# A hybrid decoder layer on one core: factor steps spread over more matrix units, gated rows in two buffers, other units in seven products, longer step counts in the retention

## The chip, the cores and the metric

The kernel runs on one core of a Trainium2 chip, in float32. The metric is the device time of one execution in microseconds (us). Five engines work at once, each with an instruction stream of its own: TensorE (PE, the matrix products; PEld is its weight loading), VectorE (DVE), ScalarE (ACT), GpSimd (POOL) and SyncE (SP, whose queue issues nearly all transfers). In the code they are `PE`, `V`, `A`, `G_` and `SP`. An instruction waits until what it reads has been written and what it overwrites has been read; those behind it on its engine wait too.

## What is computed

520 columns go through one layer: 512 prompt tokens and 8 single-token samples.

```python
proj = rmsnorm(x) @ w_in                        # q, k, v, g of the retention; q, k, v of the attention; two gates
o_r  = retention(rotary(q_r), rotary(k_r), v_r) # 4 heads, 256 wide keys, 512 wide values; state S = gamma*S + k^T v
a    = (group_norm(o_r) * silu(g_r)) @ w_pa
b    = dilated_attention(q_a, k_a, v_a) @ w_pb  # 12 heads
h    = x + (sigmoid(gate_a) * a + sigmoid(gate_b) * b) @ w_o
u, w = split(rmsnorm(h) @ w_ffn_in)             # hidden width 2816 = 22 blocks of 128
y    = rmsnorm(h + (silu(u) * w) @ w_ffn_out)
```

For each of the 8 samples the retention also reads its state (256 x 512 in each of the 4 heads), updates it and writes it back.

## The kernel before

**Columns and products.** Activations stand transposed: features on the 128 partitions, 520 columns along the free dimension, in two halves of 260 (`HF`). Each float32 factor is split in a high part (ACT, a copy to the matrix format) and a low part (DVE, the difference), and a product is three matmuls: high by high, high by low, low by high. Weights come as a stream `wall` of 512 KB pieces in the order of use (line 167). Each block of 512 columns of weights is split by `block_hi`: high part `wh` on ACT (line 200), low part `wl` on DVE (line 203); `advance` keeps this five blocks ahead of the product.

**Units.** `unit` (line 250 for its matmuls) makes one block of 128 output rows: for each of the k blocks of its input, 3 matmuls for each half, and then one `pump()`. The results of consecutive units lie in two pairs of accumulator banks (`pm`), so a unit can start when the results of the unit before the last one have been read.

**Seven-product units.** `quad` (line 306 for its matmuls) makes two output blocks, over two input halves and two column halves, by seven block products where the plain way has eight. For this it needs sums of weight blocks (`qq`, lines 184 to 190, on DVE) and seven factors of the input. Each of its seven steps has 12 matmuls and two pumps, so a quad has 14 pumps. The results of some steps are copied out by ACT (line 312, tiles `s12` and `s35`) and put together by DVE.

**Pumps.** There is no scheduler: instructions stand on each engine in the order in which Python issues them. Side work is written as generators in queues: P (first), S and Q. Each pump first runs the calls that `later(n, ...)` put off by n pumps, and then takes one step of those queues that stand in the current entry of `pattern`: with `["PS", "P", "PS"]` the P queue steps at each pump and the S queue at two of three. A `yield` ends a step. The number of yields thus sets how much other work, and how many matmuls, lie between two pieces of side work.

**Retention.** Per head h, the units are q (2), k (2), and then g (4) and v (4), for heads 0 and 3 v before g. On the P queue run `gen_scores` (the split of q and k, lines 490 and 491; the score matmuls, line 503; the decay factor, line 510), `gen_vT` and `gen_out` (the products with v, line 551; normalisation; the final state, line 569). On the S queue runs `gen_sample`: sixteen steps for the 8 samples and two halves of the state, each with an ACT product `kv` (line 619), a DVE update `st` (line 654), every other one with a DVE product `y` (line 635), loads of `state` (line 606) and of `vb` (line 611) and a store (line 624); after eight steps, and after sixteen, the `y` go through matmuls into `oacc` (line 664). The sample work of head h is started at the end of its v units, so that of head 2 runs beside the units of head 3.

**Feed forward.** 22 input units, `FFSEQ` in order; with unit i go the weights of both halves of SwiGLU. A plain one (`ffn_in`) is two units of 8 input blocks (16 pumps); those in `INQ` are quads (`ffn_in_quad`). After unit 8 and after unit 16 come four output quads (`ffn_out`), which use the gated rows of units 0 to 7, and 8 to 15; the rows of units 16 to 21 are used as they are at the end. The first three plain units use rows that aren't yet normed (`X2`); their results are multiplied with the row factor `rs2` (lines 1320 and 1329). The others use `XP`, and the quads also `XT`: these are the factors, which `gen_factors` makes on the P queue from the start of the feed forward. It makes the 8 blocks of `XP` (lines 1217, 1220, 1221) with two yields each, and then four groups of `XT` (lines 1232 to 1244) with six yields, the last one with five. The gated rows of a pair of units go to `UF` (`middle`; lines 1333 and 1360), one buffer; `right`, on the S queue, makes seven factors of them for the output quads (lines 1292 to 1303). `right` of the pair (0, 1) is pushed at unit 2 and is run to its end at once there (`finish`), because unit 2 writes to the same buffer; the other pairs' is pushed at the end of the odd unit and runs beside the unit after it.

Of the kernel before, what the change touches and what calls it, by code (L numbers as in the profile page):

```python
# [8 lines left out]
F32 = mybir.dt.float32  # L9
# [15 lines left out]
CHUNKS = ((0, 8), (8, 8), (16, 6))  # L25
LAST = [(c, k) for k0 in (0, 4) for c in range(2) for k in range(k0, min(k0 + 4, 6))]
LAST[8:] = [(0, 4), (1, 4), (0, 5), (1, 5)]
INQ = (6, 7, 9, 10, 11, 13, 14, 15, 17, 18, 19, 21)
FFSEQ = []
for (a_, n_), ahead_ in zip(CHUNKS, (1, 1, 0)):  # L30
    FFSEQ += [("in", i_, i_ in INQ) for i_ in range(a_ and a_ + 1, a_ + n_ + ahead_)]
    FFSEQ += [("out", c_, True) for c_ in range(0, 8, 2) if ahead_]
QUADS = {128 + 2 * i_: 4 for i_, e_ in enumerate(FFSEQ) if e_[2]}
GAMMA = [1.0 - 2.0 ** (-5.0 - h) for h in range(RH)]


@with_exitstack
def tile_hybrid_layer(
# [411 lines left out]
    for h in range(RH):  # L450
# [31 lines left out]
        def gen_scores(h, tens, Dt):  # L482
            kt = [rp.tile([128, 4, DK], F32R, tag="kt" + i, name="kt" + i) for i in "hl"]
            tens["kt"] = kt
            q, k = tens["q"], tens["k"]
            parts = []
            for x, i in ((q, "h"), (k, "l")):
                p = rp.tile([128, 4, T], F32R, tag="v" + i, bufs=1, name="p" + i)
                hi, lo = p[:, 0:2, :], p[:, 2:4, :]
                A.activation(hi, x, AF.Copy)  # L490
                later(3, lambda x=x, hi=hi, lo=lo: V.tensor_tensor(lo, x, f32(hi), op=ALU.subtract))
                parts.append((hi, lo))
                yield
            (qh, ql), (kh, kl) = parts
            for _ in range(3 if h else 8):
                yield
            for jb in range(4):
                n = T - 128 * jb
                sp = sbank()
                i0 = min(jb * 128, HT)  # L500
                mm = [(dt, x, y) for dt in range(2) for x, y in ((kh, qh), (kh, ql), (kl, qh))]
                for i, (dt, x, y) in enumerate(mm):
                    PE.matmul(sp[:, :T - i0], x[:, dt, jb * 128:(jb + 1) * 128], y[:, dt, i0:], start=i == 0,  # L503
                              stop=i == len(mm) - 1)
                yield
                sp = sp[:, jb * 128 - i0:]
                t = tmp("sc")
                o = SCO[jb] + (128 if jb == 3 else 0)
                hi, lo = scs[0][:, o:o + n], scs[1][:, o:o + n]
                V.tensor_tensor(t[:, :n], sp[:, :n], Dt[:, :n], op=ALU.mult)  # L510
                A.activation(hi, t[:, :n], AF.Copy)
                later(2, lambda hi=hi, lo=lo, t=t, n=n: V.tensor_tensor(lo, t[:, :n], f32(hi), op=ALU.subtract))
            tens["v"] = [rp.tile([128, 4, DV], F32R, tag="v" + i, bufs=1, name="v" + i) for i in "hl"]
            for jp in range(2):
                sp = sbank()
                for i in range(2):
                    for dt in range(2):
                        jb = 2 * jp + i
                        pe_T(sp[:, i * 256 + dt * 128:i * 256 + dt * 128 + 128], k[:, dt, jb * 128:(jb + 1) * 128])
                yield  # L520
                for i in range(2):
                    jb = 2 * jp + i
                    A.activation(kt[0][:, jb, :], sp[:, i * 256:(i + 1) * 256], AF.Copy, scale=kdec[:, h, jb:jb + 1])
                yield
                for i in range(2):
                    jb = 2 * jp + i
                    V.scalar_tensor_tensor(kt[1][:, jb, :], sp[:, i * 256:(i + 1) * 256], kdec[:, h, jb:jb + 1],
                                           f32(kt[0][:, jb, :]), op0=ALU.mult, op1=ALU.subtract)
# [13 lines left out]
        def gen_out(h, tens):  # L542
# [20 lines left out]
                                       tokv(tens["g"][:, c, :]), op0=ALU.mult, op1=ALU.mult)  # L563
            tens["gdone"] = True
            for dt in range(2):
                sp = sbank()
                for jb in range(4):
                    for x, y in three:
                        PE.matmul(sp, kt[x][:, jb, dt * 128:(dt + 1) * 128], v[y][:, jb, :], start=jb == 0 and x == y,  # L569
                                  stop=jb == 3 and x == 1)  # L570
                    if jb % 2:
                        yield
                sf = tmp("sf")
                A.activation(sf[:, :DV], sp, AF.Copy)
                yield
                later(2, lambda sf=sf, dt=dt: SP.dma_start(s_p[0, 0, h, dt * 128:(dt + 1) * 128, :], sf[:, :DV]))
# [16 lines left out]
        def gen_sample(h, tens):  # L593
# [57 lines left out]
            for i in range(2 * NS):  # L651
# [5 lines left out]
                later(1, lambda i=i, f=second if dt else first: f(i))  # L657
                yield
                if i % 8 == 7:
                    for _ in range(3):  # L660
                        yield
                    for bb in range(b - 3, b + 1):
                        j = bb % 4
                        PE.matmul(acc[32 * j:32 * j + 32, :], om[:, bb, :], ys[bb], start=b == 3, stop=b == NS - 1,  # L664
                                  tile_position=(0, 32 * j), skip_group_check=True)
                    yield
# [102 lines left out]
            g_units()  # L769
        push("P", gen_out(h, tens))  # L770
        before = tens
        pattern[:] = ["PS", "P", "PS"] if h == RH - 2 else ["P", "S", "P", "PS", "P", "S"]


    SG = {}
# [434 lines left out]

    def gen_factors():
        yield from gen_norm2()
        xs = {}

        def one(c, out):
            x = ftmp("xn")
            V.scalar_tensor_tensor(x, hT[:, c, :], g2v[:, c:c + 1], rs2, op0=ALU.mult, op1=ALU.mult)
            xs[c] = x
            hi, lo = (XP[:, i, c // 2, 1:3, :] if c % 2 else XP[:, i, c // 2, 0::3, :] for i in range(2))
            A.activation(hi, halves(x), AF.Copy)  # L1220
            later(2, lambda: V.tensor_tensor(lo, halves(x), f32(hi), op=ALU.subtract))

        for c in range(8):
            one(c, None)
            yield
            yield
        for k in range(4):
            x1, x2 = xs.get(2 * k), xs.get(2 * k + 1)
            if k < 3:
                x1, x2 = ftmp("xn"), ftmp("xn")  # L1230
                for c, x in ((2 * k, x1), (2 * k + 1, x2)):
                    V.scalar_tensor_tensor(x, hT[:, c, :], g2v[:, c:c + 1], rs2, op0=ALU.mult, op1=ALU.mult)
                yield
            t = fp.tile([128, 4, HF], F32, tag="ts", name="ts")
            V.tensor_tensor(t[:, 0, :], x1[:, :HF], x1[:, HF:], op=ALU.subtract)
            V.scalar_tensor_tensor(t[:, 1, :], x2[:, HF:], -1.0, t[:, 0, :], op0=ALU.mult, op1=ALU.subtract)
            V.tensor_tensor(t[:, 2, :], x2[:, HF:], x1[:, HF:], op=ALU.subtract)
            V.scalar_tensor_tensor(t[:, 3, :], t[:, 1, :], -1.0, x2[:, :HF], op0=ALU.mult, op1=ALU.subtract)
            yield
            for j in (0, 2):  # L1240
                hi, lo = XT[:, 0, k, j:j + 2, :], XT[:, 1, k, j:j + 2, :]
                A.activation(hi, t[:, j:j + 2, :], AF.Copy)  # L1242
                yield
                V.tensor_tensor(lo, t[:, j:j + 2, :], f32(hi), op=ALU.subtract)
                yield

    def xnsrc(k):
        return tuple((XP[:, i, k // 2, k % 2, :], XP[:, i, k // 2, 2 if k % 2 else 3, :]) for i in range(2))
# [8 lines left out]
    push("P", gen_factors())  # L1257

    UL = fp.tile([128, 28, HF], F32R, name="UL")
    UF = fp.tile([128, 8, HF], F32, name="UF")  # L1260
    NP = CHUNKS[2][0]
    NX = 3

    def snaps():
        return [fp.tile([128, 2, HF], F32, tag=t, bufs=b, name=t) for t, b in (("s12", 2), ("s35", 1))]

    def whole(i, t):
        hi, lo = (halves(u[:, i - NP, :]) for u in (UHp, ULp))
# [3 lines left out]
    def middle(i, mult):  # L1272

        if i > NP:
            t = halves(ftmp("fu"))
            mult(t)
            whole(i, t)
            return
        if i == NX - 1:
            rights.append(push("S", right(UF, 0)))  # L1280
        if i % 2 == 0 and rights:
            finish("S", rights[-1])
        mult(UF[:, 1:3, :] if i % 2 else UF[:, 0::7, :])
        if i % 2 and i > 1:
            rights.append(push("S", right(UF, i % 8 // 2)))

    rights = []

    def right(t, k):

        yield
        V.tensor_tensor(t[:, 3, :], t[:, 0, :], t[:, 7, :], op=ALU.subtract)
        V.scalar_tensor_tensor(t[:, 4, :], t[:, 2, :], -1.0, t[:, 3, :], op0=ALU.mult, op1=ALU.subtract)
        yield
        V.tensor_tensor(t[:, 5, :], t[:, 2, :], t[:, 7, :], op=ALU.subtract)
        V.scalar_tensor_tensor(t[:, 6, :], t[:, 4, :], -1.0, t[:, 1, :], op0=ALU.mult, op1=ALU.subtract)
        yield
        for j, n in ((0, 3), (3, 2), (5, 2)):
            hi, lo = (u[:, k, j:j + n, :] for u in (UH4, UL4))
            A.activation(hi, t[:, j:j + n, :], AF.Copy)  # L1300
            yield
            yield
            V.tensor_tensor(lo, t[:, j:j + n, :], f32(hi), op=ALU.subtract)
            yield

    def open_u():
        nonlocal UH4, UL4, UHp, ULp
# [77 lines left out]
    for kind, i, seven in FFSEQ:  # L1385
# [3 lines left out]
            ffn_out(i)  # L1389
            continue  # L1390
        if i == NP + 1:
            whole(NP, UF[:, 0::7, :])
        (ffn_in_quad if seven else ffn_in)(i)

    last = bpool.tile([128, 7 * D], F32, tag="bg", name="last")
# [216 lines left out]
```

## Time and profile before

| | us |
|---|---|
| median of 3 runs | 1319.31 (1316.19 to 1320.3) |
| the profiled execution | 1318.89 |
| its span, first to last instruction | 1317.1 |
| PE, PEld busy in the span | 1282.0, 1247.7 |
| DVE, ACT, POOL busy in the span | 820.3, 574.9, 83.2 |

In the answers about the trace a time is in us from the start of the span. A wait row names the engine, the tile and line of the waiting instruction, and behind the arrow what ended the wait; then the total, the number of waits and the longest. A row of the timeline has start, length, engine, line, operation, output and inputs, and in brackets the idle time of the engine before it. A window row has the window, its length, the busy time of each engine with the number of its instructions, the granted clock of PE (1.00 is full speed), the busy share of the transfer engines and GB/s.

### The profile page before, as it was taken

Reading aid. Unit: us, or ns where it says so; the run is one execution under the profiler, and the core shown is the slowest. Engines: PE = TensorE matmul, PEld = TensorE weight load, DVE = VectorE, ACT = ScalarE, POOL = GpSimd, SP = SyncE. Lnnn points to the kernel's source line nnn. Section 1 sums busy time; section 2 is a strip of 40 time slices with the busy share of each in tenths; the row PEclk is TensorE's granted clock in tenths of the full one; section 3 lists DMA queues with packets and bytes.
Section 4 is the critical chain, followed back from the end, with each engine's and each line's share of the span. In section 5 each row is a group of like instructions: output and inputs, shape, how many; then the busy total and the mean of one; then the engine's idle time right before and its main releaser. Section 6 shows DMA issues by size and latency. Waiting matters only on the chain.

```text
span 1317.1 us, 25670 instructions
## 1 busy us (share of the span) xinstructions
PE 1282.0 (97%) x10465; PEld 1247.7 (95%) x10465; DVE 820.3 (62%) x1735; ACT 574.9 (44%) x1100; POOL 83.2 (6%) x69
## 2 busy tenths in 40 slices
PE   8999999999999999999999999999979999999997
PEld 7999999998888999999999999899979999999997
DVE  7867636847655532234545455476697788879765
ACT  4564334534554522244434343233444556555532
POOL 3601001001002000000000000040000000000000
PEclk9999999999899999999999999999999999999999
DMA  6266235737575332445555455534222333233321
GB/s 219 83 233 228 93 113 196 245 119 233 170 267 182 95 92 87 136 126 152 157 161 164 138 173 177 204 121 128 74 62 83 97 113 113 76 101 113 97 81 66
DMA packets 89782, 183.35 MB, mean 139 GB/s; under 512 B 12024, under 2 KB 33944, under 8 KB 89664
## 3 DMA queue, kind: packets, MB, share of 16 engines
q1 hardware_dynamic: 88944, 180.64, 43.7%
q8 instruction: 82, 1.34, 0.4%
q10 hardware_dynamic: 720, 1.07, 0.2%
q14 instruction: 36, 0.29, 0.1%
HBM read 155.70 MB, written 25.98 MB: 138 GB/s over the span
## 4 chain that ended last, share of the span: by engine, by line
PE 85%; DVE 7%; DMA 2%; issue 2%; ACT 2%; POOL 1%; SPq 0%; DVEq 0%; ACTq 0%
PE pm L250 59%; PE pm L306 12%; PE sp L322 3%; PE pc L306 2%; DMA vb<-vd 2%; PE sp L551 2%; PE sp L569 2%; PE pm L1500 1%; DVE wl L203 1%; PE sp L961 1%; PE sp L503 1%; PE sp L911 1%; ACT wh L200 1%; PE oacc L664 1%; PE sacc L1106 1%
## 5 line engine op out<-in xcount | busy, mean ns | idle before, releaser
L250 PE MATMUL pm<-X,wh 128*128 128x260 f32 x3392 | 561.8, 288 | 8.1 <-ACT XT L1242 3.8
L250 PEld LDWEIGHTS pm<-X,wh 128*128 128x128 f32 x3392 | 470.2, 190 | 23.1 <-issue 8.3
L203 DVE TENSOR_TENSOR wl<-raw,wh 128x512 fp32r<-128x512 f32 x384 | 275.8, 720 | 169.6 <-ACT wh L200 165.8
L250 PE MATMUL pm<-X,wl 128*128 128x260 f32 x1696 | 342.7, 284 | 0.1
L200 ACT ACTIVATE wh<-raw 128x512 fp32r<-128x512 f32 x384 | 238.7, 625 | 211.0 <-PE pm L250 160.7
L250 PEld LDWEIGHTS pm<-X,wl 128*128 128x128 f32 x1696 | 262.9, 189 | 0.5 <-DVE wl L364 0.5
L250 PE MATMUL pm<-GA,wh 128*128 128x260 f32 x512 | 82.2, 283 | 0.0
L250 PE MATMUL pm<-XP,wh 128*128 128x260 f32 x448 | 72.2, 283 | 3.2 <-DVE fb L1329 1.9
L306 PE MATMUL pm<-XT,wh 128*128 128x260 f32 x384 | 71.9, 286 | 2.6 <-DVE UF L1360 1.7
L250 PEld LDWEIGHTS pm<-GA,wh 128*128 128x128 f32 x512 | 70.1, 189 | 0.0
L250 PEld LDWEIGHTS pm<-XP,wh 128*128 128x128 f32 x448 | 61.3, 188 | 3.6 <-issue 2.1
L306 PEld LDWEIGHTS pm<-XT,wh 128*128 128x128 f32 x384 | 59.1, 188 | 4.8 <-DVE UF L1360 2.7
L619 ACT ACTIVATE kv<-vb,ks 128x512 f32<-128x512 f32 x64 | 44.2, 714 | 29.2 <-DMA vb<-vd 28.8
L331 POOL TENSOR_TENSOR r<-v,cst 128x4 f32<-128x4 f32 (+4 forms) x14 | 17.6, 1259 | 595.5 <-DVE v L329 595.5
L306 PE MATMUL pm<-UH,wh 128*128 128x260 f32 x192 | 54.2, 282 | 0.0
L306 PE MATMUL pm<-UL,wh 128*128 128x260 f32 x192 | 54.2, 282 | 0.0
L306 PE MATMUL pm<-XT,wl 128*128 128x260 f32 x192 | 54.2, 282 | 0.0
L306 PE MATMUL pm<-UH,wl 128*128 128x260 f32 x192 | 54.1, 282 | 0.0
L654 DVE SCALAR_TENSOR_TENSOR st<-st,kv 128x512 f32<-128x512 f32 x64 | 45.4, 713 | 11.4 <-ACT kv L619 11.4
L250 PE MATMUL pm<-GA,wl 128*128 128x260 f32 x256 | 51.6, 283 | 0.0
L312 ACT ACTIVATE s<-pm 128x260 f32<-128x260 f32 x80 | 30.8, 386 | 45.6 <-PE pm L306 45.3
L200 ACT ACTIVATE wh<-qq 128x512 fp32r<-128x512 f32 x60 | 37.3, 629 | 30.4 <-PE pm L250 17.4
(322 smaller groups left out, 2100.1 us busy)
## 6 DMA issues: line engine op xcount, KB each, us to landing
raw<-wall SPq DMA_DIRECT2D x192, 512.0 KB
st<-state SPq DMA_DIRECT2D x64, 256.0 KB
out<-st SPq DMA_DIRECT2D x64, 256.0 KB
area<-ck SPq DMA_DIRECT2D x24, 512.0 KB
vb<-vd SPq DMA_DIRECT2D x32, 256.0 KB
area<-qd SPq DMA_DIRECT2D x12, 512.0 KB
cb<-cd SPq DMA_DIRECT2D x4, 768.0 KB
xr<-xT SPq DMA_DIRECT2D x8, 260.0 KB
```

The costliest lines, as they stand in the source:

```text
L200: A.activation(h, r, AF.Copy)
L203: V.tensor_tensor(l, r, f32(h), op=ALU.subtract)
L250: PE.matmul(pm[:, f, :HF], w, x[f] if isinstance(x, tuple) else x[:, f * HF:(f + 1) * HF], start=first, stop=last)
L306: PE.matmul(out[bank], w[:, ks], factor(i, k, x), start=bank not in begun, stop=k == nkp - 1 and w is l, skip_group_check=True)
L312: A.activation(snap[(0, 3, 1, None, 2)[j]], out[bank], AF.Copy)
L322: PE.transpose(out, in_, ident[:n, :n])
L331: G_.tensor_tensor(r[:rows, :ncol], v[:rows, :ncol], mhalf[:rows].to_broadcast([rows, ncol]), op=ALU.pow)
L503: PE.matmul(sp[:, :T - i0], x[:, dt, jb * 128:(jb + 1) * 128], y[:, dt, i0:], start=i == 0, stop=i == len(mm) - 1)
L551: PE.matmul(sp[:, i0:], v[x][:, jb, c * 128:(c + 1) * 128], scs[y][:, SCO[jb]:SCO[jb] + T - i0], start=jb == 0 and x == y, stop=jb == 3 an ...
L569: PE.matmul(sp, kt[x][:, jb, dt * 128:(dt + 1) * 128], v[y][:, jb, :], start=jb == 0 and x == y, stop=jb == 3 and x == 1)
L619: A.activation(kvs[i][:, :DV], vbs[b], AF.Copy, scale=ks[:, dt, b:b + 1])
L654: V.scalar_tensor_tensor(sts[i], sts[i], GAMMA[h], kvs.pop(i)[:, :DV], op0=ALU.mult, op1=ALU.add)
```

## The change

- `INQ`: the seven-product input units are 7, 8, 9, 11, 12, 13, 15, 16, 17, 19, 20, 21 in place of 6, 7, 9, 10, 11, 13, 14, 15, 17, 18, 19, 21: twelve as before. Units 8 and 16, ahead of the output quads, become quads; 6, 10, 14 and 18 become plain.
- `gen_factors`: four yields for each block of `XP` in place of two; thirteen for each group of `XT` in place of six; the last group makes its two normed rows again, as the others do, in place of keeping them.
- `UF`: two buffers of four rows in turn in place of one of eight, and a tile `us` for the four sums that `right` makes; `right` of (0, 1) isn't run to its end at unit 2 any more; one DVE operation to a step, and fewer yields for the last pair of a set of eight (k = 3). `s12` has one buffer in place of two.
- Retention: `gen_scores` waits 7, 7 and 6 steps in heads 1, 2, 3 in place of 3 before its matmuls (head 0: 8 as before); `gen_out` has one more yield ahead of each half of the final state; `gen_sample` has five yields ahead of the `oacc` matmuls in place of three; and beside the units of head 3 the S queue steps at three of four pumps in place of two of three.

```diff
-INQ = (6, 7, 9, 10, 11, 13, 14, 15, 17, 18, 19, 21)
+INQ = (7, 8, 9, 11, 12, 13, 15, 16, 17, 19, 20, 21)
+SCW = (8, 7, 7, 6)
...
-            for _ in range(3 if h else 8):
+            for _ in range(SCW[h]):
                 yield
...
             for dt in range(2):
+                yield
                 sp = sbank()
...
                 if i % 8 == 7:
-                    for _ in range(3):
+                    for _ in range(5):
                         yield
...
-        pattern[:] = ["PS", "P", "PS"] if h == RH - 2 else ["P", "S", "P", "PS", "P", "S"]
+        pattern[:] = ["PS", "PS", "P", "PS"] if h == RH - 2 else ["P", "S", "P", "PS", "P", "S"]
...
         for c in range(8):
-            one(c, None)
-            yield
-            yield
+            one(c)
+            for _ in range(4):
+                yield
         for k in range(4):
-            x1, x2 = xs.get(2 * k), xs.get(2 * k + 1)
-            if k < 3:
-                x1, x2 = ftmp("xn"), ftmp("xn")
-                for c, x in ((2 * k, x1), (2 * k + 1, x2)):
-                    V.scalar_tensor_tensor(x, hT[:, c, :], g2v[:, c:c + 1], rs2, op0=ALU.mult, op1=ALU.mult)
+            x1, x2 = ftmp("xn"), ftmp("xn")
+            for c, x in ((2 * k, x1), (2 * k + 1, x2)):
+                V.scalar_tensor_tensor(x, hT[:, c, :], g2v[:, c:c + 1], rs2, op0=ALU.mult, op1=ALU.mult)
                 yield
...
+            yield
             V.tensor_tensor(t[:, 2, :], x2[:, HF:], x1[:, HF:], op=ALU.subtract)
             V.scalar_tensor_tensor(t[:, 3, :], t[:, 1, :], -1.0, x2[:, :HF], op0=ALU.mult, op1=ALU.subtract)
+            yield
             yield
             for j in (0, 2):
                 hi, lo = XT[:, 0, k, j:j + 2, :], XT[:, 1, k, j:j + 2, :]
                 A.activation(hi, t[:, j:j + 2, :], AF.Copy)
                 yield
+                yield
                 V.tensor_tensor(lo, t[:, j:j + 2, :], f32(hi), op=ALU.subtract)
                 yield
+            yield
+            yield
...
+        if i % 2 == 0:
+            if len(rights) > 1:
+                finish("S", rights[-2])
+            UF[i // 2] = fp.tile([128, 4, HF], F32, tag="uf", bufs=2, name="uf")
+        t = UF[i // 2]
+        mult(t[:, 1:3, :] if i % 2 else t[:, 0::3, :])
         if i == NX - 1:
-            rights.append(push("S", right(UF, 0)))
-        if i % 2 == 0 and rights:
-            finish("S", rights[-1])
-        mult(UF[:, 1:3, :] if i % 2 else UF[:, 0::7, :])
-        if i % 2 and i > 1:
-            rights.append(push("S", right(UF, i % 8 // 2)))
+            rights.append(push("S", right(UF[0], 0)))
+        if i % 2 and i > NX - 1:
+            rights.append(push("S", right(t, i % 8 // 2)))
...
+        t = fp.tile([128, 4, HF], F32, tag="us", name="us")
+        V.tensor_tensor(t[:, 0, :], b[:, 0, :], b[:, 3, :], op=ALU.subtract)
+        yield
...
+        for x, j, n in ((b[:, 0:3], 0, 3), (t[:, 0:2], 3, 2), (t[:, 2:4], 5, 2)):
             hi, lo = (u[:, k, j:j + n, :] for u in (UH4, UL4))
-            A.activation(hi, t[:, j:j + n, :], AF.Copy)
-            yield
-            yield
-            V.tensor_tensor(lo, t[:, j:j + n, :], f32(hi), op=ALU.subtract)
-            yield
+            A.activation(hi, x, AF.Copy)
+            yield
+            if k < 3:
+                yield
+            V.tensor_tensor(lo, x, f32(hi), op=ALU.subtract)
+            if k < 3:
+                yield
```

More of the change, by code (lines that the diff above doesn't have):

```diff
@@ L1212, in gen_factors, with one @@
         yield from gen_norm2()
-        xs = {}
-        def one(c, out):
+        def one(c):
             x = ftmp("xn")
             V.scalar_tensor_tensor(x, hT[:, c, :], g2v[:, c:c + 1], rs2, op0=ALU.mult, op1=ALU.mult)
-            xs[c] = x
             hi, lo = (XP[:, i, c // 2, 1:3, :] if c % 2 else XP[:, i, c // 2, 0::3, :] for i in range(2))
@@ L1259, in tile_hybrid_layer @@
     UL = fp.tile([128, 28, HF], F32R, name="UL")
-    UF = fp.tile([128, 8, HF], F32, name="UF")
+    UF = {}
     NP = CHUNKS[2][0]
@@ L1264, in snaps @@
     def snaps():
-        return [fp.tile([128, 2, HF], F32, tag=t, bufs=b, name=t) for t, b in (("s12", 2), ("s35", 1))]
+        return [fp.tile([128, 2, HF], F32, tag=t, bufs=b, name=t) for t, b in (("s12", 1), ("s35", 1))]
     def whole(i, t):
@@ L1278, in middle, with right @@
             return
-        if i == NX - 1:
-            rights.append(push("S", right(UF, 0)))
-        if i % 2 == 0 and rights:
-            finish("S", rights[-1])
-        mult(UF[:, 1:3, :] if i % 2 else UF[:, 0::7, :])
-        if i % 2 and i > 1:
-            rights.append(push("S", right(UF, i % 8 // 2)))
+        if i % 2 == 0:
[4 more added lines that the diff above has]
+        mult(t[:, 1:3, :] if i % 2 else t[:, 0::3, :])
+        if i == NX - 1:
+            rights.append(push("S", right(UF[0], 0)))
+        if i % 2 and i > NX - 1:
+            rights.append(push("S", right(t, i % 8 // 2)))
     rights = []
-    def right(t, k):
+    def right(b, k):
         yield
-        V.tensor_tensor(t[:, 3, :], t[:, 0, :], t[:, 7, :], op=ALU.subtract)
-        V.scalar_tensor_tensor(t[:, 4, :], t[:, 2, :], -1.0, t[:, 3, :], op0=ALU.mult, op1=ALU.subtract)
+        t = fp.tile([128, 4, HF], F32, tag="us", name="us")
+        V.tensor_tensor(t[:, 0, :], b[:, 0, :], b[:, 3, :], op=ALU.subtract)
         yield
-        V.tensor_tensor(t[:, 5, :], t[:, 2, :], t[:, 7, :], op=ALU.subtract)
-        V.scalar_tensor_tensor(t[:, 6, :], t[:, 4, :], -1.0, t[:, 1, :], op0=ALU.mult, op1=ALU.subtract)
+        V.scalar_tensor_tensor(t[:, 1, :], b[:, 2, :], -1.0, t[:, 0, :], op0=ALU.mult, op1=ALU.subtract)
         yield
-        for j, n in ((0, 3), (3, 2), (5, 2)):
+        V.tensor_tensor(t[:, 2, :], b[:, 2, :], b[:, 3, :], op=ALU.subtract)
+        yield
+        V.scalar_tensor_tensor(t[:, 3, :], t[:, 1, :], -1.0, b[:, 1, :], op0=ALU.mult, op1=ALU.subtract)
+        yield
+        for x, j, n in ((b[:, 0:3], 0, 3), (t[:, 0:2], 3, 2), (t[:, 2:4], 5, 2)):
             hi, lo = (u[:, k, j:j + n, :] for u in (UH4, UL4))
-            A.activation(hi, t[:, j:j + n, :], AF.Copy)
+            A.activation(hi, x, AF.Copy)
             yield
-            yield
-            V.tensor_tensor(lo, t[:, j:j + n, :], f32(hi), op=ALU.subtract)
-            yield
+            if k < 3:
[3 more added lines that the diff above has]
+                yield
     def open_u():
@@ L1391, in tile_hybrid_layer @@
         if i == NP + 1:
-            whole(NP, UF[:, 0::7, :])
+            whole(NP, UF[NP // 2][:, 0::3, :])
         (ffn_in_quad if seven else ffn_in)(i)
```

## The prediction, written before the changed kernel had run

> **What bounds the kernel now.** I read the page's busy times first. PE is busy for nearly the whole span and the change takes no matmul away (twelve seven-product units before and after, the same shapes), so only PE's idle time and its slow clock can be won.
>
> ```profile
> span 1317.1 us, 25670 instructions
> PE 1282.0 (97%) x10465; PEld 1247.7 (95%) x10465; DVE 820.3 (62%) x1735; ACT 574.9 (44%) x1100; POOL 83.2 (6%) x69
> ```
>
> 35.1 us of the span are idle. The timeline of PE alone, with the waits of its lines, places the part that the change can reach. In the retention of head 3 these are the waits over 0.5 us:
>
> ```profile
> 323.27 1.04 PE L664 MATMUL oacc<-y,om 128*32 128x512 f32 x2 [0.53 <-DVE y L635]
> 330.48 0.50 PE L503 MATMUL sp<-ph,pl 128*128 128x512 f32 x1 [0.92 <-ACT pl L490]
> 331.98 0.53 PE L503 MATMUL sp<-ph,pl 128*128 128x512 f32 x1 [1.00 <-DVE ph L491]
> 333.72 2.08 PE L503 MATMUL sp<-ph,pl 128*128 128x512 f32 x4 [1.21 <-DVE pl L491]
> 389.53 1.05 PE L664 MATMUL oacc<-y,om 128*32 128x512 f32 x2 [1.64 <-DVE y L635]
> 406.01 0.50 PE L569 MATMUL sp<-vh,kth 128*128 128x512 f32 x1 [1.06 <-DVE GT L562]
> ```
>
> Together 6.36 us. In the feed forward the table of waits has, first for its start (940 to 1010 us), then for the quads (1009 to 1265 us):
>
> ```profile
> PE pm L250 <- ACT XT L1242: 3.8, 1, 3.8
> PE pm L250 <- DVE fb L1329: 1.9, 1, 1.9
> PE pm L250 <- ACT fa L1323: 1.3, 1, 1.3
> ```
>
> ```profile
> PE pm L306 <- DVE fa L1352: 2.1, 3, 0.8
> PE pm L306 <- DVE UF L1360: 1.7, 3, 0.6
> PE pm L306 <- ACT s L312: 0.7, 2, 0.4
> ```
>
> 7.0 us at the start, 4.5 us in the quads. The third loss shows only in short windows: PE is busy, but on a slow clock (the column before the last two).
>
> ```profile
> 332.00:334.00 2.00, 0.79 (x2) 0.45 (x3) 2.00 (x3) 0.89 (x2) 0.00 (x0) 0.58 0.90 267
> 334.00:336.00 2.00, 2.00 (x6) 1.63 (x7) 1.70 (x4) 0.00 (x0) 0.00 (x0) 0.50 0.95 217
> 336.00:338.00 2.00, 2.00 (x10) 2.00 (x9) 1.21 (x2) 1.60 (x3) 0.00 (x0) 0.50 1.03 396
> 338.00:340.00 2.00, 2.00 (x13) 2.00 (x12) 0.88 (x2) 1.15 (x3) 0.00 (x0) 0.72 0.77 293
> ```
>
> ```profile
> 964.00:966.00 2.00, 2.00 (x10) 2.00 (x11) 2.00 (x4) 0.22 (x1) 0.00 (x0) 0.50 0.12 8
> 966.00:968.00 2.00, 2.00 (x14) 2.00 (x13) 2.00 (x4) 0.00 (x0) 0.00 (x0) 0.70 0.76 246
> ```
>
> Busy time by the missing share of the clock is what it costs: 0.79 x 0.42 + 1.0 + 1.0 + 2.0 x 0.28 = 2.9 us behind the score stalls, and 1.0 + 0.6 = 1.6 us behind the stall of 3.8 us. So about 22.4 us are within reach.
>
> **Start of the feed forward.** Why PE waits there is read from DVE's groups of 940 to 1010 us: L1217 to L1244 are the factors (the two sums not shown, L1235 and L1238, have 1.7 us each as well).
>
> ```profile
> L203 DVE TENSOR_TENSOR wl<-raw,wh 128x512 fp32r<-128x512 f32 x18 | 12.2, 688 | 6.1 <-ACT wh L200 6.1
> L1217 DVE SCALAR_TENSOR_TENSOR xn<-hT,vec,rs 128x520 f32<-128x520 f32 x8 | 6.0, 756 | 0.0
> L1221 DVE TENSOR_TENSOR XP<-xn,XP 128x520 fp32r<-128x520 f32 x8 | 5.6, 700 | 1.9 <-ACT XP L1220 1.4
> L1244 DVE TENSOR_TENSOR XT<-ts,XT 128x520 fp32r<-128x520 f32 x8 | 5.3, 696 | 0.0
> L1303 DVE TENSOR_TENSOR UL<-UF,UH 128x520 fp32r<-128x520 f32 (+1 forms) x6 | 4.5, 783 | 0.0
> L1232 DVE SCALAR_TENSOR_TENSOR xn<-hT,vec,rs 128x520 f32<-128x520 f32 x6 | 4.3, 754 | 0.0
> L1333 DVE TENSOR_TENSOR UF<-pm,fa 128x520 f32<-128x520 f32 x3 | 2.1, 699 | 3.3 <-PE pm L250 3.3
> L1236 DVE SCALAR_TENSOR_TENSOR ts<-xn,ts 128x260 f32<-128x260 f32 x4 | 1.7, 428 | 0.1
> L1237 DVE TENSOR_TENSOR ts<-xn 128x260 f32<-128x260 f32 x4 | 1.7, 423 | 0.0
> ```
>
> A plain unit of the feed forward, and quads, in windows of their own:
>
> ```profile
> 1031.40:1042.90 11.50, 11.50 (x98) 11.50 (x98) 8.95 (x17) 5.52 (x10) 0.00 (x0) 1.00 0.24 79
> 1073.00:1083.10 10.10, 10.10 (x86) 10.10 (x85) 9.19 (x17) 5.54 (x11) 0.00 (x0) 1.00 0.38 105
> 1083.10:1093.20 10.10, 10.10 (x87) 10.10 (x85) 8.40 (x15) 5.72 (x12) 0.00 (x0) 1.00 0.34 104
> 1093.20:1104.90 11.70, 10.64 (x85) 10.02 (x83) 11.28 (x22) 6.93 (x14) 0.00 (x0) 1.00 0.31 92
> ```
>
> A plain unit takes 11.5 us and has 16 pumps: 0.72 us to a pump. The factors are 6.0 + 5.6 + 4.3 + 4 x 1.7 + 5.3 = 28.0 us of DVE, on 8 x 2 + 3 x 6 + 5 = 39 pumps, 28.1 us of PE. They alone fill DVE, and beside them a unit needs 4 x 0.69 us of `wl` and up to three results at 0.70 us: 4.9 us, 0.42 of its time. So DVE gets some 28.1 x 0.42 = 11.8 us behind, the reads of PE's banks stand in its queue behind factors, and PE waits until they come: 7.0 us of stalls and 1.6 us of clock. (The row that names ACT and XT is such a wait: the bank is free when DVE's `fb` comes behind two `xn` and four sums.)
>
> The change puts the factors on 8 x 4 + 4 x 13 = 84 pumps, 60.5 us, and adds two `xn` (1.5 us): 29.5 us, half of DVE. Units 1 and 2 then need 4.9 us and 16/4 x (0.756 + 0.700) = 5.8 us: 10.7 of 11.5. Units 3 and 4 need 2.75 + 0.70, 16/13 of a group (2 x 0.754 + 4 x 0.425 + 2 x 0.696 = 4.6) = 5.7, and one `right` (4 x 0.425 + 0.96 + 2 x 0.69 = 4.1; 0.96 is 3 x 783 less two of 0.69, as half of the six of L1303 are two sets): 13.2 us of 11.5. That leaves DVE 3.4 us behind; a bank may be late by one unit, 5.75 us, before PE waits. So I take 0.7 us of new stalls, between 0 and 3.4. Nothing needs the factors earlier: `XP` is complete at pump 14 + 32 and first read at pump 48 (its first block was made at pump 15), `XT` at pump 98 and first read at pump 112, which leaves 10 us. If that cover goes, unit 7 waits. **Gain 8.6 - 0.7 = 7.9 us.** Running `right` of the first pair at ease instead of at once takes 4.1 us out of unit 2, where two of the stalls are, and is in this.
>
> **Quads.** The third window of the four is a quad with no `right` beside it, the fourth one with: DVE busy 8.40 and 11.28 us where PE needs 10.1. Only the latter makes PE wait. Before, that is units 6, 10 and 14, 1.5 us for each of the three (4.5 in the table). After, `right` of (6, 7), (10, 11) and (14, 15) runs beside units 8, 12 and 16, which are now quads; 3, 4, 6, 10 and 14, beside which the other five run, are plain. So three stay three. Behind 8 and 16 now come output quads, where DVE has 9.19 of 10.1 us (second window): it can get back 0.9 us in each, so I take 0.5 us of loss for this, between 0 and 2. The finer steps of `right` move no DVE time. The one buffer of `s12` costs nothing: its last reader is the very DVE read of the bank that the next quad waits for. **Loss 0.5 us.**
>
> **Retention.** The scores of head 3 would have started at 329.56 and waited 3.13 us for the split of k. DVE made this without a pause from the end of the k unit on:
>
> ```profile
> 325.26 0.70 DVE L470 TENSOR_TENSOR rc<-pm,tr 128x520 f32<-128x520 f32 x1 [1.44 <-PE pm L250]
> 332.45 1.22 DVE L491 TENSOR_TENSOR pl<-kT,pl 128x1024 fp32r<-128x1024 f32 x1
> ```
>
> Three more steps are three pumps, 2.2 us. The third matmul is the first that needs the low part of k; two of 512 columns go before it (98 of 260 columns take 11.5 us in the plain unit, so 0.23 us each). It comes at 329.56 + 2.2 + 0.46 = 332.2 and waits until 333.7, 1.5 us. The split is issued where it was, and the S queue at three of four pumps puts the same three updates ahead of it, or one more with its `y`, 1.4 us. So 1.5 us stay (0 to 2.9) and 1.6 go. With stalls of this size the clock does not fall: around the 1.9 us wait in the feed forward it reads 1.00.
>
> ```profile
> 976.00:980.00 4.00, 2.12 (x19) 1.94 (x17) 3.96 (x10) 2.11 (x4) 0.00 (x0) 1.00 0.01 4
> 980.00:984.00 4.00, 4.00 (x36) 4.00 (x35) 3.97 (x8) 1.60 (x4) 0.00 (x0) 1.00 0.00 0
> ```
>
> So the 2.9 us of slow clock go as well. The Trainium skill ("TensorE: Matmul & The Clock Gate", "Why this matters for your kernels") puts the fall to half speed down to idle gaps of PE over some 3 us. The trace agrees for the gap of 3.8 us, but not around 332 us, where the longest single gap is 1.21 us; so the measurement decides, and by the rule alone the 2.9 us would not be won.
>
> Two more yields ahead of `oacc` and the faster S queue: the first `oacc` of a head comes after 2 + 6 + 1 + 8 + 3 yields, at S step 21, which is 21 / (2/3) = 31.5 pumps, and after the change at step 23, 23 / (3/4) = 30.7 pumps; its last `y` is at step 17, 25.5 and 22.7 pumps. The slack grows from 6 to 8 pumps, 1.4 us; that removes the 0.53. The 1.64 follow late `vb` transfers, whose issue moves little: I take 0.4 of them. One yield ahead of line 569 gives 0.7 of 1.06. The table of waits has one more at the scores, of 0.4 us (1.6 less the 1.2 above), in head 2, and the longer count there covers it:
>
> ```profile
> PE sp L503 <- DVE pl L491: 1.6, 2, 1.2
> ```
>  **Gain 1.6 + 2.9 + 0.5 + 0.4 + 0.7 + 0.4 = 6.5 us**, less 0.4 for side work that now lies later, as `gen_out` by six steps: 6.1.
>
> **Sum.** 7.9 - 0.5 + 6.1 = 13.5. The profiled execution's 1318.89 is 0.4 under the median of 1319.31, and its span 1.8 below its time; from the median, 1319.3 - 13.5 = 1305.8, about 1306. A measurement of this kernel can tell 0.3%, 4 us, from no change: faster is below 1315.3, slower above 1323.3.
>
> **Rivals.** (1) The scores keep their stall and the slow clock. For it: the split of k is bound by DVE, and the faster S queue brings DVE more. Against: PE comes 2.2 us later. It takes back 1.6 + 2.9: 1310. The Trainium skill's gap rule above, by which only the 2.9 us would stay, would give 1309. (2) DVE's arrears in units 3 and 4 reach PE (2.7 more), and the output quads pay their 2 (1.5 more), with some of it on a slow clock (1.6): 1312. (3) All stalls in reach go, those of the quads too: 1319.3 - 22.4 = 1297. Against: three quads with `right` remain. (4) The waits only move to other places, since DVE and ACT have the same work: 1319. For it: nothing but order changes; against: at the start of the feed forward DVE's load falls from over 1.4 to about 1. (5) Slower: behind units 8 and 16 no plain unit gives DVE time, and its arrears go through all eight output quads and units 9 and 17. Each then pays the 1.5 us and 0.42 for the second read of a bank that an output quad needs (the 128x260 shape of L1237): 10 x 1.9 = 19 us, 1306 + 19 = 1325. It decides where arrears of a quad with `right` pass the 0.9 us that an output quad gives back; against it, PE's own stall ends the arrears each time.
>
> **How the numbers follow.** Forecast 0.54, (1) 0.17, (2) 0.10, (3) 0.06, (4) 0.07, (5) 0.06. The range 1299 to 1314 leaves out (3), (4) and (5), 0.19. Faster: the first four cases, 0.87, less 0.04 for the ends of (1) and (2) above 1315: 0.83. Same: 0.07 + 0.04 = 0.11. Slower 0.06.
>
> **What would show it.** Right: no PE wait over 1 us between 940 and 1010 us, clock 1.00 there; one wait of about 1.5 us at line 503 in head 3 with the clock at 1.00; three groups of waits at line 306, behind units 8, 12 and 16. Wrong: waits at line 250 beside units 3 to 5, clock under 0.9 near 335 us, or line 306 waits in the output quads.

## The result and the profile after

The changed kernel takes 1307.06 us (median of 4 runs, 1304.41 to 1307.51) where the kernel before takes 1319.8 (4 runs beside it): ratio 0.9899, 95% interval 0.9868 to 0.993, 12.7 us less. A second set on another chip gave 0.9911 (0.9896 to 0.9925). The forecast was 1306.

Span and PE line of its page:

```profile
span 1305.4 us, 25694 instructions
PE 1277.5 (98%) x10465; PEld 1245.1 (95%) x10465; DVE 820.5 (63%) x1737; ACT 573.6 (44%) x1100; POOL 83.6 (6%) x69
```

PE has its 10465 matmuls as before, and 27.9 us without work in place of 35.1. The waits over 0.15 us between the start of head 3's scores and the end of the quads, from the timeline of PE (the lines have moved: 503 is now 504, 664 is 666, 569 is 571, 306 is 307):

```profile
332.28 1.19 PE L504 MATMUL sp<-ph,pl 128*128 128x512 f32 x4 [1.23 <-DVE pl L492]
338.84 0.98 PE L504 MATMUL sp<-ph,pl 128*128 128x256 f32 x6 [1.43 <-DVE sc L511]
382.64 1.04 PE L666 MATMUL oacc<-y,om 128*32 128x512 f32 x2 [0.51 <-DVE y L637]
400.39 0.50 PE L571 MATMUL sp<-vh,kth 128*128 128x512 f32 x1 [0.20 <-DVE GT L563]
408.35 1.04 PE L666 MATMUL oacc<-y,om 128*32 128x512 f32 x2 [1.75 <-DVE y L637]
...
938.98 0.71 PE L251 MATMUL pm<-X,wh 128*128 128x260 f32 x4 [0.53 <-DVE fa L1331]
1030.04 0.39 PE L307 MATMUL pm<-UH,wh 128*128 128x260 f32 x1 [1.40 <-DVE fa L1363]
1032.29 0.39 PE L307 MATMUL pm<-UH,wh 128*128 128x260 f32 x1 [0.55 <-DVE uf L1371]
1114.26 0.51 PE L307 MATMUL pm<-XP,wh 128*128 128x260 f32 x2 [0.79 <-DVE fa L1363]
1117.13 0.52 PE L307 MATMUL pm<-XT,wh 128*128 128x260 f32 x2 [1.16 <-DVE uf L1371]
1159.33 0.39 PE L307 MATMUL pm<-UH,wh 128*128 128x260 f32 x1 [1.40 <-DVE fa L1363]
1161.59 0.39 PE L307 MATMUL pm<-UH,wh 128*128 128x260 f32 x1 [0.56 <-DVE uf L1371]
```

The stalls of 3.8, 1.9 and 1.3 us at the start of the feed forward are gone; the row at 938.98 is a wait of 0.5 us at unit 1 that stood there before too (942.46). Three groups of waits in the quads remain, 1.95 us each by their rows, behind units 8, 12 and 16. In head 3 the wait for the split of k has shrunk, and two have come that weren't there: the scores' fourth block (338.84) and the second `oacc` (408.35).

The row of that 0.5 us wait makes a good mark, since the work on both sides of it is the same in both kernels: up to it 942.46 us before and 938.98 after, from it to the end of the span 374.6 and 366.4. So 8.2 us of the gain lie behind the mark, in the feed forward, and 3.5 ahead of it. (The span after holds 1.6 us of slow clock ahead of the mark, in head 0, which the span before doesn't; more on this below.)

DVE in the plain units 2 to 6, in windows of 11.5 us:

```profile
950.00:961.50 11.50, 11.50 (x98) 11.50 (x97) 9.82 (x15) 4.94 (x10) 0.00 (x0) 1.00 0.27 90
961.50:973.00 11.50, 11.50 (x99) 11.50 (x97) 10.94 (x21) 6.50 (x12) 0.00 (x0) 1.00 0.29 91
973.00:984.50 11.50, 11.50 (x99) 11.50 (x98) 11.47 (x22) 6.00 (x10) 0.00 (x0) 1.00 0.32 93
984.50:996.00 11.50, 11.50 (x99) 11.50 (x98) 11.43 (x22) 5.26 (x9) 0.00 (x0) 1.00 0.39 99
996.00:1007.50 11.50, 11.50 (x99) 11.50 (x98) 9.37 (x17) 4.82 (x8) 0.00 (x0) 1.00 0.17 57
```

DVE (the fourth time of a row) is full for some 23 us, in units 4 and 5, and PE (the second) still has no idle time. How far behind DVE is shows in its timeline: it reads the results of units 3 and 4 (line 1344) at 977.39 and 988.52, that is 3.8 and 3.4 us after their last matmuls (unit 3 begins with the first matmul on `XP`, at 962.1, and takes 11.5 us). Arrears shorter than the 5.75 us of one call of `unit` cost nothing here.

### The profile page after: what moved, and what is told of

Read it like the earlier page. It is cut to its first block, busy times and chain, and to the rows that moved or that the text cites. A ratio compares the mean times of both kernels' runs of the same rounds, so it can differ in the third digit from the quotient of the medians.

```text
span 1305.4 us, 25694 instructions
## 1 busy us (share of the span) xinstructions
PE 1277.5 (98%) x10465; PEld 1245.1 (95%) x10465; DVE 820.5 (63%) x1737; ACT 573.6 (44%) x1100; POOL 83.6 (6%) x69
## 4 chain that ended last, share of the span: by engine, by line
PE 85%; DVE 6%; DMA 4%; issue 2%; ACT 2%; POOL 1%; SPq 1%; DVEq 0%; ACTq 0%
PE pm L251 61%; PE pm L307 10%; PE sp L323 3%; DMA out<-st 2%; PE pc L307 2%; PE sp L552 2%; DVE wl L204 1%; PE sp L571 1%; PE pm L1511 1%; PE sp L963 1%; PE sp L504 1%; DMA vb<-vd 1%; ACT wh L201 1%; PE sp L913 1%; DVE st L656 1%
```

## The experiments

The theory: each part is worth the waits and the slow clock of its own stage, and the parts add up. The rival: the waits only move to the next reader of DVE's queue.

**The two halves.** `ret_only` is the kernel before with all the edits of the retention, `ff_only` the changed kernel with the retention as before.

```diff
-            for _ in range(3 if h else 8):
+            for _ in range(SCW[h]):
...
             for dt in range(2):
+                yield
...
-                    for _ in range(3):
+                    for _ in range(5):
...
-        pattern[:] = ["PS", "P", "PS"] if h == RH - 2 else ...
+        pattern[:] = ["PS", "PS", "P", "PS"] if h == RH - 2 else ...
```

> The kernel before with only the retention's edits (the longer step counts, the yields in gen_out and ahead of oacc, the faster S queue). Theory (the parts add up; each is worth the waits and the slow clock of its own stage): the retention takes 3 to 4.6 us less, the feed forward's start keeps its waits of 7.0 us and its slow clock of 1.6 us, the quads their 4.5 us; 1315 to 1317 us from a median of 1319.8. Rival (the waits only move on to the next reader): under 1 us of gain, 1319 us.

> The changed kernel with the retention as before: only the feed forward's edits. Theory: waits of 6.4 us and a slow clock of 2.9 us in the retention of head 3 come back, the feed forward stays as in the changed kernel, gain 7 to 8.5 us: 1311 to 1313 us. Rival (the feed forward's part only pays with the retention's): gain under 4 us.

Measured: `ret_only` 1314.34 us, ratio 0.9968 (0.9957 to 0.998); `ff_only` 1310.76, 0.9941 (0.9928 to 0.9954); the kernel before beside both 1318.43. So 4.1 and 7.7 us, 11.8 together, against 12.7 for the whole change, whose interval reaches from 9 to 17 us: within the noise the halves add up. From the mark to the end of the span `ret_only` takes 374.7 us, as before, and `ff_only` 366.3, as after.

**Factors as dense as before, all else changed.**

```diff
         for c in range(8):
             one(c)
-            for _ in range(4):
+            for _ in range(2):
                 yield
...
                 V.scalar_tensor_tensor(x, hT[:, c, :], g2v[:, c:c + 1], rs2, op0=ALU.mult, op1=ALU.mult)
-                yield
+            yield
...
-            yield
             V.tensor_tensor(t[:, 2, :], x2[:, HF:], x1[:, HF:], op=ALU.subtract)
             V.scalar_tensor_tensor(t[:, 3, :], t[:, 1, :], -1.0, x2[:, :HF], op0=ALU.mult, op1=ALU.subtract)
             yield
-            yield
...
                 A.activation(hi, t[:, j:j + 2, :], AF.Copy)
                 yield
-                yield
                 V.tensor_tensor(lo, t[:, j:j + 2, :], f32(hi), op=ALU.subtract)
                 yield
-            yield
-            yield
```

> The changed kernel with the factors as dense as before (two yields to a block, six to a group), all else as changed, also the first quad at unit 7 and right of the first pair at ease. Theory (DVE has 28 us of factors in 28 us of PE time): of the 8.6 us of waits and slow clock at the start of the feed forward 6 to 8.6 come back, with a wait over 3 us and a clock near 0.5 behind it: 1313 to 1316 us. Rival (the burst of right at unit 2 and the early quad 6 made the waits, the spread of the factors little): under 3 us come back, 1307 to 1310 us.

Measured: 1313.55 us, 0.9966 (0.9954 to 0.9979); from the mark to the end 374.6 us, the whole gain of the feed forward lost again. Its table of waits for the start of the feed forward, and two windows behind the longest wait:

```profile
PE pm L251 <- ACT XT L1240: 3.8, 1, 3.8
PE pm L251 <- DVE fb L1335: 1.9, 1, 1.9
PE pm L251 <- DVE fa L1326: 0.5, 1, 0.5
PE pm L251 <- ACT fa L1329: 0.4, 1, 0.4
```

```profile
956.00:958.00 2.00, 1.29 (x6) 1.33 (x7) 1.97 (x4) 1.14 (x2) 0.00 (x0) 0.66 0.00 0
958.00:960.00 2.00, 2.00 (x11) 2.00 (x11) 2.00 (x4) 0.00 (x0) 0.00 (x0) 0.50 0.56 113
```

The first two waits are the old ones, and the slow clock costs 1.5 us where it cost 1.6. Only the third wait fell, from 1.3 to 0.4: that much must come from the other edits here, the `right` of the first pair, which no longer runs all at once, or the later first quad; which of them wasn't tried. The rest is the density of the factors.

**Which units are quads.** `even_plain` has quads only where no `right` runs beside them, `two_even` has two beside one.

```diff
-INQ = (7, 8, 9, 11, 12, 13, 15, 16, 17, 19, 20, 21)
+INQ = (7, 9, 11, 13, 15, 17, 18, 19, 20, 21)              # even_plain
+INQ = (7, 9, 10, 11, 13, 14, 15, 17, 18, 19, 20, 21)      # two_even
```

> The changed kernel with quads only where no right runs beside them: 7, 9, 11, 13, 15 and 17 to 21, ten in place of twelve. Theory (a quad with right beside it costs 10.1 us and 1.95 us of waits, more than a plain unit's 11.5 us): the 5.9 us of waits at the three quads go, two more plain units cost 2 x 1.4 = 2.8 us, 3.1 us are gained on the changed kernel: 1304 us. Rival (the waits come from the run of quads, whatever runs beside them): waits at line 307 behind 11, 13, 15 or in the run 17 to 21, 1308 to 1310 us.

> The changed kernel with the quads at 7, 9, 10, 11, 13, 14, 15 and 17 to 21: twelve as in it, but plain units at 8, 12 and 16 and quads at 10 and 14 beside a right. Theory: two groups of waits at line 307, behind 10 and 14, 1.7 to 2 us each, in place of three; no waits in the output quads; 2 to 2.5 us less than the changed kernel, and about 1 us more than with ten quads and none beside a right. Rival (the number of quads decides, not what runs beside them): as the changed kernel.

Measured: `even_plain` 1300.34 us, 0.9865 (0.9852 to 0.9878); `two_even` 1305.34, 0.9902 (0.9884 to 0.9919), where the changed kernel on the same chip has 0.9911. The waits in the quads of `two_even`:

```profile
1088.75 0.50 PE L307 MATMUL pm<-XP,wh 128*128 128x260 f32 x2 [0.79 <-DVE fa L1363]
1091.62 0.51 PE L307 MATMUL pm<-XT,wh 128*128 128x260 f32 x2 [1.17 <-DVE uf L1371]
1133.18 0.51 PE L307 MATMUL pm<-XP,wh 128*128 128x260 f32 x2 [0.79 <-DVE fa L1363]
1136.05 0.51 PE L307 MATMUL pm<-XT,wh 128*128 128x260 f32 x2 [1.16 <-DVE uf L1371]
```

They stand behind units 10 and 14 only; `even_plain` has none over 0.1 us. So what runs beside a quad decides where the rows stand. From the mark to the end: 366.4 (changed), 364.9 (`two_even`), 362.2 (`even_plain`). The gain of `two_even` is clear there but not in its times.

That `even_plain` gained 4.2 us and not 3.1 is explained by the times of the quads, from the start of the first matmul of one to that of the next. A quad behind a plain unit, with no `right` beside it, takes 10.07 us. The three around unit 12 of the changed kernel take 32.97, 2.76 more than three such quads, where the rows show 1.95. And the number in a row does count, though no row shows it: the five quads 17 to 21 of `even_plain` take 52.85 us, 10.07 for the first and 10.7 for each that follows, and three in a row without a `right` (19 to 21 of the changed kernel) take 31.46. Of the 2.76 us, 1.5 thus come with the `right` and the rest with the two quads that follow another. Why a wait costs more than its row is measured below.

In the times `even_plain` is 6 us ahead of the changed kernel. The code up to the mark is the same; its profiled execution came there 2.8 us earlier than that of the changed kernel, with 1.6 us less of slow clock, and 3.3 us earlier than the one of `after_again`, with 3.3 us less.

**The changed kernel again**, for the comparisons on its chip:

> The changed kernel again, beside the others on this chip. Theory: 1306 to 1308 us; the same waits as in its first profile (line 307 5.9 us, lines 504, 571 and 666 in head 3 together 5 us), and 0 to 1.6 us of slow clock behind the wait of 1.8 us at the scores of head 0, as the clock gate happens to see it.

Measured: 1306.66 us. From the mark to the end 366.2 us, the same waits in the quads (5.8 us); before the mark there were 1.5 us of slow clock in head 0 and 1.7 us behind the second `oacc`.

**The parts of the retention.** `scw_only` is the kernel before with the step counts ahead of the scores alone, `s_only` with the S queue's two edits alone, `ret_no_rate` with all but the faster S queue.

```diff
-            for _ in range(3 if h else 8):
+            for _ in range(SCW[h]):                       # scw_only, ret_no_rate
...
+                yield                                     # gen_out: ret_no_rate
...
-                    for _ in range(3):
+                    for _ in range(5):                    # s_only, ret_no_rate
...
-        pattern[:] = ["PS", "P", "PS"] if h == RH - 2 else ...
+        pattern[:] = ["PS", "PS", "P", "PS"] if h == RH - 2 else ...   # s_only
```

> The kernel before with the longer step counts ahead of the scores alone (7, 7, 6). Theory: the three waits of 3.1 us at line 503 in head 3 fall to 1.2 to 1.6 us and the clock stays at 1.00 behind them, 0.4 us go in head 2, the waits at lines 664 and 569 stay; 4 to 5 us of gain: 1314 us. Rival (the faster S queue is what moves the sample work off the scores): the slow clock stays, under 2 us of gain.

> The kernel before with the faster S queue beside head 3 and the five yields ahead of oacc alone; the scores' step counts and gen_out as before. After the run with the step counts alone (no gain, its waits moved from line 491 to line 510), theory: the two edits need each other. Alone, this one takes the 0.5 us at line 664 of head 2 away, PE still comes to the scores of head 3 before their split is done: about 3 us of waits at line 503 and the slow clock behind them stay; 0 to 1.5 us of gain. Rival (the S queue's edits are the whole gain): 3 to 4 us of gain and no wait over 1.5 us at line 503.

> The kernel before with all the retention's edits but the faster S queue (two of three pumps stay beside head 3). Theory (what counts is when the last sample updates of head 2 are issued, against the scores of head 3): the sample's second eight steps come later by two yields, the decay factor of the scores stands behind them, waits at line 503 of 3 to 5 us with a slow clock as with the step counts alone: within 1.5 us of the kernel before. Rival (the yields ahead of oacc are enough): 3 to 4 us of gain.

Measured: `scw_only` 1320.13 us, 1.0015 (1.0004 to 1.0025); `s_only` 1317.59, 0.9999 (0.9988 to 1.001); `ret_no_rate` 1314.92, 0.9971 (0.9956 to 0.9985). Neither the step counts nor the S queue's edits gain anything alone; of the step counts 4 to 5 us had been expected. In `s_only` PE still waits 3.2 us for the split of head 3, with a slow clock behind, as expected. The waits at the scores of `scw_only` (its profiled execution is its slowest, 1323.5 us), and from DVE's timeline how the longest came about:

```profile
250.73 1.29 PE L504 MATMUL sp<-ph,pl 128*128 128x256 f32 x6 [2.33 <-DVE sc L511]
336.28 1.21 PE L504 MATMUL sp<-ph,pl 128*128 128x512 f32 x4 [1.24 <-DVE pl L492]
345.13 1.65 PE L504 MATMUL sp<-ph,pl 128*128 128x256 f32 x6 [3.73 <-DVE sc L511]
```

```profile
340.47 1.31 DVE L655 SCALAR_TENSOR_TENSOR st<-st,kv 128x512 f32<-128x512 f32 x2 [2.38 <-ACT kv L620]
343.05 0.17 DVE L735 COPY vs<-pm 128x8 f32<-128x8 f32 x1 [1.27 <-ACT vT L734]
343.13 0.74 DVE L636 SCALAR_TENSOR_TENSOR y<-st,qs,y 128x512 f32<-128x512 f32 x1
343.79 0.68 DVE L204 TENSOR_TENSOR wl<-raw,wh 128x512 fp32r<-128x512 f32 x1
344.39 0.68 DVE L511 TENSOR_TENSOR sc<-sp,Dt 128x512 f32<-128x512 f32 x1
```

The fourth score block needs the bank of the first, which L511 reads. Three pumps later, L511 stands in DVE's queue behind a sample update that waits for ACT and behind the results of the first v unit (L735), which wait for ACT as well. The wait for the split shrank as forecast, and another of 3.73 us took its place. With the yields ahead of `oacc` and in `gen_out` as well, the times fall by 3 to 4 us, with or without the faster S queue; the expectation for `ret_no_rate` was wrong in that. Which of the two is the partner of the step counts wasn't tried, and its profiled execution, its slowest (1316.32 us, waits of 3.2 and 2.7 us in head 3 with a slow clock behind both), doesn't show where the gain of its median is. That stays open.

**Less time for DVE in the output quads** (fifth rival), by two operations of 128x520 that only write a tile which nothing reads any more:

```diff
+            if j == 1:
+                for _ in range(2):
+                    V.tensor_tensor(halves(rs2), h2, h2, op=ALU.add)
```

> The changed kernel with two more DVE operations of 128x520 (0.7 us each, into a tile that nothing reads any more) in each of the eight output quads. Theory (an output quad leaves DVE 0.9 us, DVE then has 10.6 us in 10.1): waits at line 307 inside the run of output quads, 0.5 us in each after the first, 2 to 5 us in all. Rival (the splits of weights are issued five blocks ahead and take it up): no wait inside the run, the same time.

One execution: 1308.49 us; from the mark to the end 371.3 us, 4.9 more than the changed kernel. One output quad of each, the changed kernel first, and the table of waits over the run of four with the added work:

```profile
1053.10:1063.20 10.10, 10.10 (x87) 10.10 (x86) 9.12 (x16) 5.53 (x12) 0.00 (x0) 1.00 0.31 110
```

```profile
1050.10:1060.83 10.73, 10.55 (x85) 10.16 (x85) 10.35 (x19) 5.65 (x12) 0.00 (x0) 1.00 0.33 99
```

```profile
PE pm L307 <- DVE hT L1395: 0.7, 4, 0.2
```

9.12 us of DVE in 10.1 is no loss; with 10.35 the quad is 10.73 long. The rows, though, show 0.2 us of waiting to a quad, while it is 0.63 longer: the end of a matmul is modelled, and covers a part of each wait. The starts show how much. Behind the wait of 1.40 us at 1030.04 in the changed kernel, two matmuls start 1.67 us later than at the usual 0.117 us from start to start (98 matmuls in 11.5 us), so a wait costs some 0.27 us more than its row, and one under 0.16 us has no row at all.

**A better version.** `best2` adds to the ten quads a longer count in head 3, `best3` a middle one with the gap behind the second score block.

```diff
-SCW = (8, 7, 7, 6)
+SCW = (8, 7, 7, 9)                                        # best2
+SCW = (8, 7, 7, 7)                                        # best3
...
-                    for _ in range(5):
+                    for _ in range(8 if h == RH - 1 else 5):             # best2
+                    for _ in range(8 if h == RH - 1 and i > 8 else 5):   # best3
...
+                if h == RH - 1 and jb == 1:               # best3, end of the loop over score blocks
+                    yield
+                    yield
```

> The ten quads of before (none beside a right), and in the retention 9 steps ahead of the scores of head 3 in place of 6, and 8 yields ahead of oacc in head 3 in place of 5. Theory (PE comes 2.2 us later to the scores, when DVE has the split and the first decay factor done; 2.2 to 2.9 us later to oacc): the waits at line 504 in head 3 (1.2 and 1.5 us) and at line 666 (0.8 and 1.5 us) go, 4 to 5 us less than with the ten quads alone: 1296 us. Rival (DVE is short of time there, and the waits move to the products with v or to the next unit): under 2 us.

> The ten quads with none beside a right, and in head 3 7 steps ahead of the scores, two more yields behind their second block, and 8 yields in place of 5 ahead of the second oacc. Theory: waits at line 504 of 0.5 us (split) and 0 to 0.5 us (decay factor) in place of 1.2 and 1.5, 0.8 at the first oacc stays, none at the second: 2 to 4 us under the ten quads alone, 1296 to 1298 us. Rival (DVE's sample work moves the wait on again): 1299 to 1301 us.

Measured: `best2` 1298.36 us, 0.985 (0.9833 to 0.9867); `best3` 1296.87, 0.9841 (0.9823 to 0.986), faster than both kernels of this study. In `best2` the waits for the split and at `oacc` are gone, but the fourth block waits 2.4 us for L511 (1.6 with the ten quads alone), and a new wait of 1.4 us for ACT's line 749 has come at 382.11: the gain on the ten quads is 2 us in place of 4 to 5, and the rival was right. In `best3` the table of waits has these three for head 3, the first less the 1.8 us of head 0:

```profile
PE sp L504 <- DVE sc L511: 1.9, 2, 1.8
...
PE sp L504 <- DVE pl L492: 0.7, 1, 0.7
...
PE oacc L669 <- DVE y L640: 0.5, 1, 0.5
```

1.4 us in place of 5.2 with the ten quads alone.

## Why the prediction was right, and where it wasn't

*Start of the feed forward.* Right in mechanism: 7.0 us of waits and 1.6 us of slow clock gone, and all but some 1 us of them back with the old density. The 0.7 us of new stalls didn't come. DVE's arrears were there, in units 4 and 5 rather than 3 and 4: up to 3.8 us, where the sum had 3.4, and under the 5.75 us that it allowed. The size was a little short: measured by the units' starts this part is worth 9.3 us where 7.9 were forecast, because a wait costs more than its row.

*Quads.* Three stayed three, behind the units named, and the output quads had no waits of their own, so neither the second nor the fifth rival came. By the rows the price rose from 1.5 to 1.95 us each, 5.9 in all where 4.5 stood before. The times of the quads say otherwise: three in a row with one `right` take 32.96 us before (9 to 11) and 32.97 after (11 to 13); the table only counted three waits there before and two after. What did grow is the first group, behind unit 6 before and unit 8 now: measured in the same way its stall takes 1.8 us before and 2.75 now, when it runs on into the first output quad. All quads together take 1.1 us longer (210.0 and 211.1), where a loss of 0.5 was taken. Feed forward in all: 7.4 forecast, 8.2 measured (9.3 less 1.1).

*Retention.* The sum had 6.1 us; alone the part gave 4.1, and 3.5 in the profiled execution of the whole change. The waits of heads 2 and 3 fell only from 6.8 to 5.1 us. The step that failed is "Three more steps are three pumps, 2.2 us": the wait that it priced fell to 1.23 (forecast 1.5), but the sum took no account of the steps behind the first score block. They moved by three pumps too, past the first v unit's results, and the step counts alone gained nothing. The fourth block's wait of 1.43 us is for the same reader: L511 runs only at 338.10 in DVE's timeline, behind these results and a row of sample updates, which no longer wait for ACT. The second failure is `oacc`: the first one's wait fell from 1.64 to 0.51, more than forecast, but the second got 1.75; ahead of it a sample step on ACT waits 5.7 us for a `vb` transfer, to 396.60, and why this `oacc` now comes earlier (405.54, before 412.51) wasn't followed. Line 571 (0.20) and head 2 (none) came as forecast.

*The clock.* The 2.9 us behind head 3's scores went, as forecast; none of the seven profiles with just these edits of the retention has a slow clock there. But 2.9 was the figure of one execution: with the same waits `ff_only` loses 1.7 us there, and a part of the 2 us that the sum had too much may be this. And the sentence "With stalls of this size the clock does not fall" is wrong as a rule. The scores of head 0, which no edit touches, wait 1.7 to 1.8 us in each of the 14 profiled executions; the clock behind them falls in seven and holds in seven. Before and after:

```profile
60.00:62.00 2.00, 1.83 (x16) 1.86 (x17) 1.90 (x6) 1.53 (x4) 0.00 (x0) 1.00 0.68 242
```

```profile
60.00:62.00 2.00, 2.00 (x11) 2.00 (x11) 1.90 (x6) 1.35 (x3) 0.00 (x0) 0.50 0.79 254
```

In the profiled execution after, that cost 1.6 us by chance (2.0 x 0.50 here, the rest in the windows beside it).

*Sum.* 13.5 forecast, 12.7 measured: too little by 0.8 in the feed forward and too much by 2 in the retention, which partly cancelled. That the total came so close is luck in this part. Of the rivals, the first came in part (the wait moved on, the clock did not fall), the second, third and fourth did not.

## What to carry to other kernels

Where one engine makes the operands of another, compare its work per stretch of the other's time before spreading or crowding steps: 28 us of DVE on 28 us of PE cost 8 us here, on 60 us nothing. A step that is moved in an in-order queue takes all its followers past other work with it; count what the last of them lands behind, not only the first. Put the cheaper variant of a unit where the engine that feeds it has the least else to do: ten well placed quads beat twelve. Price a stall from the starts of the work on both sides of it, and not from the idle rows alone.

## What the runs showed of the hardware

An idle time of 1.7 to 1.8 us at one and the same place (head 0's scores) halves the clock of PE in seven of 14 executions and not in the others; the waits of 3.8 us did so in all six profiles that have them, no single wait of under 1.6 us did, and one of 2.4 us in `best2` did not. Three waits of 0.9 to 1.2 us within 4 us did so too (`before`, `ff_only`). The Trainium skill ("TensorE: Matmul & The Clock Gate", "What's actually happening") has PE's activity watched in a window of about 3.4 us that runs free; a fall that comes and goes at the same wait fits this, though no run here shows the window itself. The rule of the same page ("Why this matters for your kernels") to keep idle gaps under some 3 us is too wide here. Each such fall costs 1.4 to 2.9 us. The single executions of one kernel scatter by 1.6 to 7.5 us, and the slower ones tend to have the lower mean clock: the kernel before, in one set, reaches from 1315.9 us at 0.995 to 1320.35 us at 0.992.

A wait row of PE is too short: in the output quads with added work 0.2 us of rows stood for 0.63 us of time, and an input quad behind another takes 0.6 us longer with no row over 0.1 us.
